# Row softmax on one core: the first two loads as one DMA each on SyncE's queue, instead of one on SyncE's and a 128/126/2-partition split on ScalarE's

## The chip, the cores and the metric

One core of a Trainium2 chip. The metric is the device time of one execution in microseconds (us), the median over the runs. Faster or slower asks for 2%. A profile is a trace of one execution; its span (first to last instruction) is about 1.4 us shorter than the device time (158.6 of 160.00 us for the kernel before).

## The reference

```
x: 16 x 1024 x 512, float32
x_scaled = x / 2.0
e = exp(x_scaled - max(x_scaled, last axis))
return e / sum(e, last axis)
```

16,384 rows of 512 values. 33.55 MB are read and 33.55 MB written, and each value gets a maximum, an exponential with its sum, and a multiplication.

## The kernel before

One tile is `r` rows for each of the 128 partitions; consecutive rows of a partition lie together in memory, so a load or store of a tile moves one piece of r x 2,048 bytes for each partition (the trace has 128 packets of 6,144 B for tile 0's load, 128 of 30,720 B for one of 15 rows). The ten tiles have 3, 7, 13 and then seven times 15 rows. They live in one arena of 98 rows, so tiles 8 and 9 take the place of tiles 0 to 3 and are loaded only after those are stored.

```
PLAN = [
    ([3], 0), ([4, 3], 3), ([5, 4, 4], 10), ([5] * 3, 23), ([5] * 3, 38), ([5] * 3, 53),
    ([5] * 3, 68), ([5] * 3, 83), ([5] * 3, 0), ([5] * 3, 15),
]
ARENA = 98
LAG = 2
SPREAD = 1
# ... cut ...
            if t == 0:
                nc.sync.dma_start(out=sb(t), in_=dram(xf, t)).then_inc(ld[t], 16)
            elif t == SPREAD:
                r = tiles[t][1] - 1
                for p, q, lo, hi in ((0, P, 0, r), (0, 126, r, r + 1), (126, P, r, r + 1)):
                    nc.scalar.dma_start(
                        out=sb(t)[p:q, lo:hi], in_=dram(xf, t)[p:q, lo:hi]
                    ).then_inc(ld[t], 16)
            else:
                nc.scalar.dma_start(out=sb(t), in_=dram(xf, t)).then_inc(ld[t], 16)
```

VectorE works in chunks (the inner lists of PLAN): the maximum of chunk k, then the multiplication of chunk k - LAG. SyncE stores a tile when its last chunk is multiplied. The loads of tiles 0 and 1 are issued ahead of the barrier that opens the program.

```
        for k in range(len(chunks) + LAG):
            if k < len(chunks):
                do_max(k)
            if k >= LAG:
                do_mul(k - LAG)
        for t in range(len(tiles)):
            nc.sync.wait_ge(s_mul, last_chunk[t] + 1)
            nc.sync.dma_start(out=dram(of, t), in_=sb(t)).then_inc(
                st[t] if t in awaited else s_end, 16
            )
```

Of the kernel before, what the change touches and what calls it, by code (L numbers as in the profile page):

```python
# [14 lines left out]
ARENA = 98  # L15
LAG = 2

SPREAD = 1

AFTER = {8: 4, 9: 5}  # L20

# [7 lines left out]
def kernel(  # L29
# [5 lines left out]
    nc = tc.nc  # L35
# [4 lines left out]
    xf = x.flatten_outer_dims()  # L40
    of = out.flatten_outer_dims()
    N, D = xf.shape
    P = nc.NUM_PARTITIONS
# [10 lines left out]
    tiles, chunks, base = [], [], 0  # L54
    for t, (cs, at) in enumerate(PLAN):
        r = sum(cs)
# [8 lines left out]
    def dram(ap, t):  # L65
        b, r, _ = tiles[t]
        return ap[b * P : (b + r) * P].rearrange("(p r) d -> p r d", r=r)

    def sb(t):
        _, r, at = tiles[t]  # L70
        return arena[:, at : at + r, :]
# [9 lines left out]
    ld = [nc.alloc_semaphore(f"ld{t}") for t in range(len(tiles))]  # L81
# [10 lines left out]
    s_max = nc.alloc_semaphore("s_max")  # L92
# [5 lines left out]
    def issue_loads(begin, end):  # L98


        for t in range(begin, end):
            if t in behind:
                continue
            if t == 0:
                nc.sync.dma_start(out=sb(t), in_=dram(xf, t)).then_inc(ld[t], 16)
            elif t == SPREAD:

                r = tiles[t][1] - 1
                for p, q, lo, hi in ((0, P, 0, r), (0, 126, r, r + 1), (126, P, r, r + 1)):
                    nc.scalar.dma_start(  # L110
                        out=sb(t)[p:q, lo:hi], in_=dram(xf, t)[p:q, lo:hi]
                    ).then_inc(ld[t], 16)
            else:
                nc.scalar.dma_start(out=sb(t), in_=dram(xf, t)).then_inc(ld[t], 16)

    def do_max(k):
        t, b, c, a = chunks[k]
        nc.vector.reduce_max(  # L118
            out=stats[:, b : b + c],
            in_=arena[:, a : a + c],  # L120
            axis=mybir.AxisListType.X,
            negate=True,
        )._wait_ge(ld[t], 48 if t == SPREAD else 16).then_inc(s_max, 1)

    def do_mul(k):
        t, b, c, a = chunks[k]
# [20 lines left out]
    def compute_and_store():  # L147
# [6 lines that stand above are left out]
# [73 lines left out]
    entry.instructions = []  # L227
    nc.switch_bb("main", None)
    issue_loads(0, 2)
    first = list(entry.instructions)  # L230
    at = next(k for k, i in enumerate(head) if type(i).__name__ == "InstDrain")
    entry.instructions = head[:at] + first + head[at:]
    act = []
    entry.instructions = list(entry.instructions) + [i for i in jumps if i not in act]
    nc.switch_body(here, parent=None, valid_engines=[i.engine for i in jumps])
    issue_loads(2, len(tiles))
    compute_and_store()

# [29 lines left out]
```

## Time and profile before

| | before |
|---|---|
| time, median of the first 3 runs | 160.02 us (159.97 to 160.12) |
| span of the profiled run | 158.6 us |
| VectorE / ScalarE busy | 131.4 / 94.4 us |
| moved by DMA | 67.13 MB, 423 GB/s over the span |

Read the busy times against the span first: no compute engine fills it. Then look at the row of DMA slices, which does. The lines are in the prediction below. The trace also records every DMA packet (queue, start, duration, size), though not the engine that moved it. On one engine a packet starts a few ns before the end of the one ahead (30,720 B packets take 1,138 ns and follow each other every 1,134), so the 16 engines can often be told apart as 16 chains; where two chains meet, they can't.

### The profile page before, as it was taken

The numbers are of one execution on the slowest core, as the hardware profiler recorded it, in microseconds if no ns is written. First come the engines' busy times: TensorE is split into PE (matmuls) and PEld (weight loads), VectorE is DVE, ScalarE is ACT, GpSimd is POOL, SyncE is SP. The second block draws the span as 40 slices with busy tenths as digits, with TensorE's granted clock in tenths as the row PEclk, the third lists the DMA queues.
The fourth block names the chain that finished last, engine by engine and source line by source line (L and its number), as shares of the span: only waits on it lengthen the run. The fifth ranks groups of instructions, "written<-read, shape, count | busy, mean of one in ns | idle before, by whom it ended". The sixth has DMA issues, their size and how long they took to land.

```text
span 158.6 us, 621 instructions
## 1 busy us (share of the span) xinstructions
DVE 131.4 (83%) x155; ACT 94.4 (60%) x257; POOL 0.2 (0%) x4
## 2 busy tenths in 40 slices
DVE  0466799999999999999999999996999389999000
ACT  0369197736874594669738797666566809763000
POOL 0000000000000000000000000000000000000000
DMA  7999999999999999999999999999999999999996
GB/s 268 449 373 430 414 431 466 435 407 399 466 443 389 434 463 448 418 444 426 442 426 434 426 426 442 426 441 411 457 395 472 395 473 395 472 395 465 395 472 263
DMA packets 3026, 67.13 MB, mean 423 GB/s; under 512 B 336, under 2 KB 336, under 8 KB 720
## 3 DMA queue, kind: packets, MB, share of 16 engines
q1 hardware_dynamic: 1584, 34.34, 50.6%
q10 hardware_dynamic: 1440, 32.77, 48.5%
q14 instruction: 2, 0.02, 0.0%
HBM read 33.55 MB, written 33.55 MB: 423 GB/s over the span
## 4 chain that ended last, share of the span: by engine, by line
DMA 52%; DVE 38%; issue 0%
DMA arena<-in_x_dram 38%; DVE stats L118 18%; DMA out_dram<-arena 14%; DVE arena L131 13%; DVE arena L138 7%; DVE recip L127 1%
## 5 line engine op out<-in xcount | busy, mean ns | idle before, releaser
L118 DVE TENSOR_REDUCE stats<-arena 128x5 f32<-128x2560 f32 (+2 forms) x27 | 72.2, 2676 | 14.6 <-DMA arena<-in_x_dram 14.6
L176 ACT ACTIVATE arena<-arena,stats 128x512 f32<-128x512 f32 x68 | 48.2, 710 | 23.4 <-DVE stats L118 23.4
L211 ACT ACTIVATE arena<-arena,stats x60 | 42.5, 710 | 20.7 <-ACTq L203 20.7
L138 DVE TENSOR_SCALAR arena<-arena,recip 128x512 f32<-128x512 f32 x93 | 38.6, 482 | 0.7
L131 DVE TENSOR_TENSOR arena<-arena,recip 128x2560 f32<-128x2560 f32 (+2 forms) x8 | 19.9, 2491 | 0.3
L176 ACT ACTIVATION_READ_ACCUMULATOR arena<-arena,stats 128x1 f32 x68 | 12.7, 187 | 0.0
L211 ACT ACTIVATION_READ_ACCUMULATOR arena<-arena,stats x60 | 11.2, 187 | 0.0
L127 DVE RECIPROCAL recip<-stats 128x5 f32<-128x5 f32 (+2 forms) x27 | 4.8, 177 | 0.0
L171 ACT ACT_TABLE_LOAD x1 | 1.3, 1283 | 5.7 <-issue 5.7
L252 POOL MEMSET const-bfloat16-1.0<- 128x1 bf16 x1 | 0.1, 101 | 0.0
L252 POOL MEMSET const-uint8-127<- 128x1 uint8 x1 | 0.1, 101 | 0.0
L252 POOL MEMSET const-float32-0.0<- 128x1 f32 x1 | 0.1, 98 | 0.2 <-issue 0.2
L252 POOL MEMSET const-float32-1.0<- 128x1 f32 x1 | 0.1, 98 | 0.0
## 6 DMA issues: line engine op xcount, KB each, us to landing
arena<-in_x_dram ACTq DMA_DIRECT2D x7, 3840.0 KB, 46.6
out_dram<-arena SPq DMA_DIRECT2D x7, 3840.0 KB, 22.7
arena<-in_x_dram ACTq DMA_DIRECT2D x1, 3328.0 KB, 14.3
out_dram<-arena SPq DMA_DIRECT2D x1, 3328.0 KB, 21.1
out_dram<-arena SPq DMA_DIRECT2D x1, 1792.0 KB, 18.2
arena<-in_x_dram ACTq DMA_DIRECT2D x1, 1536.0 KB
arena<-in_x_dram SPq DMA_DIRECT2D x1, 768.0 KB, 6.2
out_dram<-arena SPq DMA_DIRECT2D x1, 768.0 KB, 15.8
```

The source lines that it names most:

```text
L118: nc.vector.reduce_max(out=stats[:, b : b + c], in_=arena[:, a : a + c], axis=mybir.AxisListType.X, negate=True,)._wait_ge(ld[t], 48 if t ...
L127: nc.vector.reciprocal(out=recip[:, b : b + c], in_=stats[:, b : b + c])._wait_ge(s_exp, k + 1).then_inc(s_rec, 1)
L131: nc.vector.tensor_mul(out=arena[:, a : a + c], in0=arena[:, a : a + c], in1=recip[:, b : b + c].unsqueeze(2).to_broadcast([P, c, D]),)._w ...
L138: ins = nc.vector.tensor_scalar_mul(out=arena[:, a + r], in0=arena[:, a + r], scalar1=recip[:, b + r : b + r + 1],)
L171: nc.scalar.preload_act_table(mybir.ActivationFunctionType.Exp)
L176: ins = nc.scalar.activation(out=arena[:, a + r], in_=arena[:, a + r], func=mybir.ActivationFunctionType.Exp, bias=stats[:, b + r : b + r ...
L211: ins = nc.scalar.activation(out=data, in_=data, func=mybir.ActivationFunctionType.Exp, bias=stat, scale=0.5, accum_out=stat,)
L252: nc = _bacc.Bacc("TRN2", target_bir_lowering=False, num_devices=1)
```

## The change

The intent: tile 0 first and undisturbed, tile 1 behind it on the same queue, and whole rows, with one DMA for each load in place of three for tile 1.

The constant SPREAD goes, and HALVES = 1 comes in its place:

```diff
             if t == 0:
+                for p in range(HALVES):          # HALVES = 1
+                    nc.sync.dma_start(
+                        out=sb(t)[p:P:HALVES], in_=dram(xf, t)[p:P:HALVES]
+                    ).then_inc(ld[t], 16)
+            elif t == 1:
                 nc.sync.dma_start(out=sb(t), in_=dram(xf, t)).then_inc(ld[t], 16)
-            elif t == SPREAD:
-                r = tiles[t][1] - 1
-                for p, q, lo, hi in ((0, P, 0, r), (0, 126, r, r + 1), (126, P, r, r + 1)):
-                    nc.scalar.dma_start(
-                        out=sb(t)[p:q, lo:hi], in_=dram(xf, t)[p:q, lo:hi]
-                    ).then_inc(ld[t], 16)
             else:
                 nc.scalar.dma_start(out=sb(t), in_=dram(xf, t)).then_inc(ld[t], 16)
@@ the wait of the maximum
-        )._wait_ge(ld[t], 48 if t == SPREAD else 16).then_inc(s_max, 1)
+        )._wait_ge(ld[t], 16 * HALVES if t == 0 else 16).then_inc(s_max, 1)
```

More of the change, by code (lines that the diff above doesn't have):

```diff
@@ L16 @@
 LAG = 2
-SPREAD = 1
+HALVES = 1
 AFTER = {8: 4, 9: 5}
```

## The prediction

> **What bounds the kernel now.** I read the page from the top: the busy shares, then the slices, then the DMA queues.
>
> ```profile
> span 158.6 us, 621 instructions
> DVE 131.4 (83%) x155; ACT 94.4 (60%) x257; POOL 0.2 (0%) x4
> ...
> DVE  0466799999999999999999999996999389999000
> ...
> DMA  7999999999999999999999999999999999999996
> ...
> DMA packets 3026, 67.13 MB, mean 423 GB/s; under 512 B 336, under 2 KB 336, under 8 KB 720
> ...
> q1 hardware_dynamic: 1584, 34.34, 50.6%
> q10 hardware_dynamic: 1440, 32.77, 48.5%
> ```
>
> No compute engine is full; VectorE has holes at the start, at slices 27 and 31 and after the last multiply. The 16 DMA engines have none between first and last slice. q1 is SyncE's queue (33.55 MB of stores and the 0.79 MB of tile 0), q10 ScalarE's (the other loads). Second view: the stretches.
>
> ```profile
> core 0: us, DVE busy (x) ACT busy (x) POOL busy (x), PEclk, DMA share, GB/s
> 0.00:1.00 1.00, 0.00 (x0) 0.00 (x0) 0.20 (x4) 1.00 0.04 6
> 1.00:3.00 2.00, 0.00 (x0) 0.00 (x0) 0.00 (x0) 1.00 0.98 338
> 3.00:20.00 17.00, 10.04 (x10) 8.71 (x22) 0.00 (x0) 1.00 1.02 422
> 20.00:60.00 40.00, 39.76 (x23) 27.53 (x76) 0.00 (x0) 1.00 1.01 431
> 60.00:126.00 66.00, 62.49 (x91) 47.11 (x130) 0.00 (x0) 1.00 1.01 433
> 126.00:157.00 31.00, 19.11 (x33) 11.07 (x32) 0.00 (x0) 1.00 1.00 431
> ```
>
> The last two columns carry it: share 1.00 or more and 431 to 433 GB/s, whether loads and stores mix (20 to 126) or stores run alone (126 to 157). So the kernel is 1.0 us to the first packet, then 67.1 MB through full DMA engines, then a landing. Only bytes, the start, the balance among the 16 engines, or a hole in the DMA can move the end. Third view: the timeline of the part that the change touches, and of the end.
>
> ```profile
> 0.00 0.38 SPq L105 DMA_DIRECT2D arena<-in_x_dram  x1
> 0.12 1.36 ACTq L110 DMA_DIRECT2D arena<-in_x_dram  x3
> ...
> 2.65 3.07 ACTq L114 DMA_DIRECT2D arena<-in_x_dram  x6
> ...
> 6.22 1.75 DVE L118 TENSOR_REDUCE stats<-arena 128x3 f32<-128x1536 f32 x1 [6.22 <-DMA arena<-in_x_dram]
> ...
> 9.27 3.94 DVE L118 TENSOR_REDUCE stats<-arena 128x4 f32<-128x2048 f32 x2 [1.30 <-DMA arena<-in_x_dram]
> ...
> 14.65 0.34 SPq L158 DMA_DIRECT2D out_dram<-arena  x1
> ...
> 16.99 2.82 DVE L118 TENSOR_REDUCE stats<-arena 128x5 f32<-128x2560 f32 x1 [2.37 <-DMA arena<-in_x_dram]
> ```
> ```profile
> 127.66 2.82 DVE L118 TENSOR_REDUCE stats<-arena 128x5 f32<-128x2560 f32 x1 [3.29 <-DMA arena<-in_x_dram]
> ```
> ```profile
> 137.64 9.67 SPq L158 DMA_DIRECT2D out_dram<-arena  x2
> ```
>
> Tile 0 can be used at 6.22, tile 1 at 9.27, tile 2 at 16.99; the first store is issued at 14.65. At the end VectorE waits 3.29 us for the last load, works 19.3 us without a pause, and the last store is issued at 146.98 (137.64 + 9.67 - 0.33). In the trace's packet records that store's first packet starts at 148.41, on the heels of the store before it. From issue to first packet on an empty queue took 1.0 us (first load: 0.00 to 1.00), so the last store could be about 0.4 us later before a hole opens: the slack at the end is small. The chain of waits passes through VectorE and two long DMAs (store of tile 3, load of tile 9); I don't take it for the bound, because those DMAs mostly stand in queues behind others: the load of tile 9 is issued at 81.5, and its first packet is at 108.8.
>
> [...] ScalarE's queue has 160 four-byte completion packets, which is 9 DMAs x 16 + 14 + 2. The odd split is thus no accident: two engines carry none of the 128 last rows of tile 1. [...] while tile 0 is stored beside a load, one engine's store packets (6,144 B) follow each other every 1.365 us, which is one of 230 ns plus one 30,720 B packet of 1,135 ns. [...]
>
> **The change part by part.**
>
> Rows. A 2,048 B packet goes out every 80 ns on its engine, a 12,288 B one every 457, a 14,336 B one (tile 1's store has them) every 531. Tile 1's load costs most engines 8 x 457 + 9 x 80 = 4.38 us before (two of them 10 rows, 4.46), and the two spared ones 8 x 457 = 3.66. After, all have 8 x 531 = 4.25. So 14 engines gain 0.13 to 0.21 and two lose 0.59; the mean gains (12 x 0.13 + 2 x 0.21 - 2 x 0.59)/16 = 0.05 us, nothing.
>
> Why it was split: in tile 0's load 14 engines start between 1.00 and 1.25 us, the other two only at 1.73 and 1.75. Behind the split the two without rows begin tile 2 at 7.69 and 7.79, the others at 7.70 to 8.27: over-compensated. After, I move these: the late two to about 8.29 and 8.40, the others to 7.57 to 8.14. The latest engine of the start goes from 8.27 to 8.40.
>
> What that does at the end: the engines' last packets end at 157.48 to 157.95, and two at 158.14 and 158.19. These two had a detour of 309 ns each (8,192 B fetches of instructions, at 28.08 and 71.28). Followed back packet by packet, with some ambiguity, they are not the spared two, which end near 157.5 to 157.6. After: fetching engines 158.19 - 0.13 = 158.06; spared ones 157.5 to 157.6 + 0.59 = 158.1 to 158.2. The latest is again about 158.15 (before 158.19). Sum: 0.0 us, at most a few tenths.
>
> Order. Tile 0 no longer shares the engines with tile 1: 8 packets of 230 ns after a slow first one end at about 3.1 (3.6 on the late two); with the 0.36 us that the last landing took before, its reduce starts near 4.0 instead of 6.22. Tile 1 follows on the same queue. ScalarE no longer issues three loads ahead of the opening barrier, where its arrival was the last (1.76 us); the six loads should be issued near 1.9 instead of 2.65, and tile 2's packets come in turn with tile 1's from about 4.5. Tile 1 then has about 5 packets left at 531 + 988 ns a turn: 7.6 us, so it lands near 13 (12.3 to 14), where it was 9.27. The reduces of tile 1 (3.94 us) and the multiply of tile 0 (1.45 us) stand before everything else on VectorE: the first store goes out near 18.6 instead of 14.65, and VectorE begins tile 2 near 18.6 instead of 16.99.
>
> Off the path: meanwhile the loads keep all engines full, so the bytes not stored from 18 to 22 us are loaded instead. VectorE's 1.6 us are absorbed by its two waits for loads (1.42 at 108 us, 3.29 at 124). The store queue starts about 4 us later, but before it had two small gaps between the first three stores (28.8 to 30.4 and 43.1 to 45.2) which more backlog closes, giving back about 2.7. Net, loads lead by a little: the last one lands about 126 instead of 127.6, and the last store is issued at 145.5 to 147. The slack at the end grows or stays; the end does not move.
>
> **The rivals.** (1) The spared engines were in fact the ones that set the end, or a fetch falls on one of them: the end is then 158.15 + 0.6, that is +0.5 us, 160.5. For it: the author went to the trouble of such a split. Against: my tracing. (2) A new wait: tile 1's delay of 4 us shifts VectorE, the last load or the last store by more than the 0.4 us of slack; each us beyond costs a us, so 161. Against: two waits of VectorE and a leading load queue lie between. (3) A hole in the DMA after tile 0, if SyncE's second DMA came too late: its issue at about 0.45 us plus 1.0 to 1.7 is before 3.1, so no. (4) A gain: the start loses 0.9 to 1.4 us on each engine against its packets' plain sum (15.1 us from the first packet to the end of tile 2, where 14.1 are accounted for), some of it while two queues mix small packets (460 to 650 ns for packets that otherwise take 460). In-order loads may save 0.2 to 0.3: 159.7.
>
> **Range and chances.** No part reaches 1 us on the path: sum 0.0, rival 1 up by 0.5, rival 4 down by 0.3; two per cent would be 3.2 us. Predicted 160.0 us, range 159.5 to 160.6; faster 0.01, within 2% 0.97, slower 0.02.
>
> **What would show it.** First reduce near 4.0, second near 13, first store near 18.6, barrier and ScalarE's loads near 1.9; DMA slices full throughout; 320 completion packets instead of 336, none of 2,048 B; last store issued no later than 147.4, its first packet directly behind the store before it; the last packets of the 16 engines ending between 157.4 and 158.3. Wrong would be: a DMA slice under 9 in the middle, a last store with a pause ahead of its packets, or one or two engines that end 0.5 us after all others.

The sum came to 0.0 us. One step rested on a rule alone: that no rate above the 433 GB/s of the middle stretch was to be had, which no run here shows. The row counts stand on the trace of before: beside nine DMAs with 16 completion packets each, ScalarE's queue has 16 more for the 126 + 2 rows, and two engines carry none of these rows (their last 12,288 B packets end at 7.684 and 7.790 us, tile 2's first ones start at 7.686 and 7.792). The ten rows on two engines are an estimate: 128 rows shared evenly by the other 14 are nine each and two over.

## The result, and the profile after

160.34 us (160.26 to 160.46, 4 runs) against 160.05 us (159.97 to 160.12, 4 runs): ratio 1.0019, 95% interval 1.0002 to 1.0037. The ratio is the mean time of one kernel's runs over that of the other's in the same rounds, so not quite the ratio of the medians. By the 2% measure it is the same time; the 0.3 us are small, but the interval leaves out 1.

The page of the changed kernel, the lines that answer to those in the prediction:

```profile
span 159.0 us, 619 instructions
DVE 131.2 (83%) x155; ACT 94.4 (59%) x257; POOL 0.2 (0%) x4
...
DVE  0405999999999999999999999999999699995000
...
DMA  7999999998999999999999999999999999999996
...
DMA packets 2882, 67.13 MB, mean 422 GB/s; under 512 B 320, under 2 KB 320, under 8 KB 576
```

The DMA row is still full, with one 8 near 38 us. VectorE now has a hole at slices 2 and 3 and fewer later. The 16 missing completion packets (320, not 336) are those of the split. The timeline of the changed kernel, its beginning and its end (start and duration in us, then what ran):

```profile
0.00 0.38 SPq L106 DMA_DIRECT2D arena<-in_x_dram  x1
...
0.43 0.42 SPq L110 DMA_DIRECT2D arena<-in_x_dram  x1
1.92 2.94 ACTq L112 DMA_DIRECT2D arena<-in_x_dram  x6
4.49 1.75 DVE L116 TENSOR_REDUCE stats<-arena 128x3 f32<-128x1536 f32 x1 [4.49 <-DMA arena<-in_x_dram]
...
13.69 3.95 DVE L116 TENSOR_REDUCE stats<-arena 128x4 f32<-128x2048 f32 x2 [7.45 <-DMA arena<-in_x_dram]
...
18.95 2.82 DVE L116 TENSOR_REDUCE stats<-arena 128x5 f32<-128x2560 f32 x1
19.06 0.35 SPq L156 DMA_DIRECT2D out_dram<-arena  x1
```
```profile
126.03 2.82 DVE L116 TENSOR_REDUCE stats<-arena 128x5 f32<-128x2560 f32 x1 [1.22 <-DMA arena<-in_x_dram]
```
```profile
136.01 9.67 SPq L156 DMA_DIRECT2D out_dram<-arena  x2
```

Tile 0 comes 1.7 us sooner (4.49, before 6.22), tile 1 comes 4.4 us later (13.69, before 9.27), and the first store goes out 4.4 us later (19.06, before 14.65). At the end it has all been made up: the last load is there at 126.03 instead of 127.66, and the last store is issued at 145.35 (136.01 + 9.67 - 0.33) instead of 146.98. Its first packet is at 148.48, 3.1 us after the issue, and the store ahead starts its last packet at 148.35, so it waited in a queue that never ran empty. Nothing on VectorE decides the end in either kernel; the DMA engines do.

So the 0.3 us must be in how the DMA engines work. The stretches of before, then of the changed kernel (stretch, length, busy times, clock; the last two columns are DMA share and GB/s):

```profile
1.00:16.00 15.00, 7.06 (x7) 7.91 (x20) 0.00 (x0) 1.00 1.01 402
16.00:46.00 30.00, 28.81 (x18) 18.92 (x53) 0.00 (x0) 1.00 1.01 430
```
```profile
1.00:16.00 15.00, 4.06 (x3) 3.51 (x7) 0.00 (x0) 1.00 1.04 431
16.00:46.00 30.00, 29.79 (x21) 21.81 (x60) 0.00 (x0) 1.00 0.99 413
46.00:157.00 111.00, 97.36 (x133) 69.09 (x190) 0.00 (x0) 1.00 1.01 434
```

The changed kernel starts better, 431 instead of 402 GB/s, and gives it back from 16 to 46 us, 413 instead of 430. The share of busy time doesn't tell it (0.99 at 413 GB/s, 1.01 at 430): a packet that takes longer counts as busy all the while. From the packet records I worked out a time lost per engine: a packet's undisturbed spacing (230 ns for 6,144 B, 531 for 14,336, 987 for 26,624, 1,134 for 30,720, 80 for 2,048) is what it should use, and what a stretch holds beyond the sum of these, over 16 engines, is lost. I also took the end of each engine's last packet.

| trace | lost 1 to 16 us | lost 16 to 46 | lost 46 to 157 | mean end | latest end |
|---|---|---|---|---|---|
| before | 1.21 | 0.29 | 0.07 | 157.74 | 158.19 |
| changed | 0.76 | 1.00 | 0.04 | 157.93 | 158.56 |

Start -0.45, middle +0.71, sum with the rest +0.23; whole rows need a little less time (0.05 us on the mean, by the same spacings), so the mean end moved by +0.19. The latest engine was 0.45 us behind the mean and is now 0.63 behind: another 0.18. Together they are the +0.37 between these two executions. (Two copies of one kernel differ too; see the repeats.)

### The profile page after: what moved, and what is told of

It is laid out like the page before. It is cut to its first block, busy times and chain, and to the rows that moved or that the text cites. A ratio compares the mean times of both kernels' runs of the same rounds, so it can differ in the third digit from the quotient of the medians.

```text
span 159.0 us, 619 instructions
## 1 busy us (share of the span) xinstructions
DVE 131.2 (83%) x155; ACT 94.4 (59%) x257; POOL 0.2 (0%) x4
## 4 chain that ended last, share of the span: by engine, by line
DMA 49%; DVE 42%; issue 0%; SPq 0%
DMA arena<-in_x_dram 35%; DVE stats L116 21%; DMA out_dram<-arena 15%; DVE arena L129 13%; DVE arena L136 7%; DVE recip L125 1%; SPq L106 0%
```

## The experiments

Theory A: only the balance counts; two engines are late by themselves, the split relieved them, and now they set the end. Theory B: the later first stores meet the loads at a worse time, and the loss in the middle is what was added. Ten kernels ran, each with 5 rounds.

**The changed kernel once more.** No edit.

> The changed kernel once more, for its interval and a second trace. In the first trace the engines' last packets end at 157.93 us on the mean (before 157.75) and the latest two at +0.63 (before +0.44). Theory A (balance: the two engines without rows in the split are late by themselves and now set the end) and theory B (the later stores make load packets run longer at 22 to 26 and 34 to 38 us: 0.3 and 0.5 us lost per engine there, where before lost 0.0 and 0.2) both expect 160.3 us. B expects the stretched packets at the same places again; if they are elsewhere or gone, B's loss is chance of one execution.

Measured 160.49 us (160.35 to 160.65) against 160.06, ratio 1.0027 (1.0014 to 1.0040). Lost 0.78, 0.95 and 0.05 in the three stretches; mean end 157.91, latest 158.62. The stretched packets are at the same places: 0.27 lost at 22 to 24 us, 0.14 and 0.38 at 34 to 38. So the loss belongs to the schedule, and the kernel is slower by 0.2 to 0.3%.

**The kernel before once more.** No edit.

> The kernel before once more, for a second trace and for how far two copies of one kernel differ in this measure. 160.05 us, ratio within 0.1%. If the time lost per engine on longer packets falls where it fell before (0.5 us between 6 and 12 us, 0.05 at 30 to 32, 0.15 at 36 to 40), it belongs to the schedule and not to one execution; the mean end of the engines is then again near 157.75 and the latest at +0.44.

Measured 160.14 us, ratio 0.9998 (0.9984 to 1.0011). Lost 1.18, 0.40 and 0.09: again at the start (0.41 between 6 and 12 us) and little in the middle. But the mean end is 157.84 and the latest 158.49, where I expected 157.75 and 158.19. Loss and its places repeat; the end of the latest engine differs by 0.3 us between two executions of one kernel. The two pairs of traces put the middle at +0.55 to +0.71 and the mean end at +0.07 to +0.19; of the latest engine's part a single trace can't be trusted to more than a sign.

**Tile 1 whole, left on ScalarE's queue** (the kernel before with one part of the change; the wait for tile 1 goes from 48 to 16 with it):

```diff
-            elif t == SPREAD:
-                ...three DMAs of 128, 126 and 2 partitions...
             else:
                 nc.scalar.dma_start(out=sb(t), in_=dram(xf, t)).then_inc(ld[t], 16)
```

> The kernel before, but tile 1 whole in one DMA, still on ScalarE's queue beside tile 0. A (balance alone): as the changed kernel, 160.3 us, the two late engines 0.6 us behind the mean. B: stores start as early as before, so no loss in the middle; mean end at 157.7, and the late pair at most at 158.2 to 158.4: 160.0 to 160.2 us.

Measured 160.13 us (160.09 to 160.53) against 160.06, ratio 1.0013 (1.0000 to 1.0026). Its stretches:

```profile
1.00:16.00 15.00, 7.06 (x7) 8.54 (x21) 0.00 (x0) 1.00 1.04 431
16.00:46.00 30.00, 29.24 (x18) 18.73 (x52) 0.00 (x0) 1.00 1.00 415
```

The time is where B put it, but not for B's reason. The start is as good as the changed kernel's: the whole tile alone brings the 431 GB/s, and the queue does nothing for it. Tile 1 can be used at 8.65 us here, at 13.69 from SyncE's queue in the changed kernel. The packets show where it was lost. With the split, the first 26,624 B packet of tile 2 took 1,341 to 1,485 ns on every engine (1,281 to 1,446 in the second trace), and 987 ns on every engine here. It is not simply the packet behind a small row that gets slow: the two engines that carry no 2,048 B row went from a 12,288 B packet straight to tile 2, and theirs took 1,485 and 1,445 ns, the longest of all. What in the split does it, the rows on the other engines or three DMAs in place of one, no run here separates. And 0.93 us are lost in the middle although the first store is issued at 14.02, as early as before. So "later stores lose more" is too simple. A doesn't hold as stated either: the latest engine was 0.41 us behind the mean (158.27 against 157.86), not 0.6. In time, this kernel and the changed one can't be told apart (1.0013 against 1.0019 and 1.0027, with intervals that overlap), so no cost of the new order alone is shown.

**The split kept, but on SyncE's queue in order** (the changed kernel with the other part undone):

```diff
             elif t == 1:
-                nc.sync.dma_start(out=sb(t), in_=dram(xf, t)).then_inc(ld[t], 16)
+                r = tiles[t][1] - 1
+                for p, q, lo, hi in ((0, P, 0, r), (0, 126, r, r + 1), (126, P, r, r + 1)):
+                    nc.sync.dma_start(
+                        out=sb(t)[p:q, lo:hi], in_=dram(xf, t)[p:q, lo:hi]
+                    ).then_inc(ld[t], 16)
```

> The changed kernel, but tile 1 is split again into 128x6 rows and 126 + 2 rows, now on SyncE's queue in order. A (balance alone): the late pair is relieved of 0.6 us, the time goes back to that of before, 160.05 us. B (later stores): the mean loss of the middle stays, and only the 0.2 us of the late pair come back: 160.15 to 160.25, mean end of the engines still near 157.9, largest deviation 0.4 or less.

Measured 164.38 us (163.68 to 165.05) against 160.06, ratio 1.0262 (1.0237 to 1.0287). Both theories missed it by 4 us, and it can't tell them apart. The page's slices of VectorE and DMA, and VectorE's timeline at tile 1:

```profile
DVE  0400049999999999999999999999999999999400
...
DMA  7999998999999999999999999999999999088988
```
```profile
22.76 3.95 DVE L120 TENSOR_REDUCE stats<-arena 128x4 f32<-128x2048 f32 x2 [16.51 <-DMA arena<-in_x_dram]
```

The small rows now stand in a queue that takes turns with the loads of tiles 2 and 3: each 2,048 B row, nine or ten on each of 14 engines, waits for a 26,624 B or 30,720 B packet (in the kernel before, too, one store packet and one load packet alternate on an engine, every 1.365 us), and the last of them ends at 21.12 us. Tile 1 can be used at 22.76 instead of 13.69. From there VectorE never rests and yet comes too late: the DMA engines stand still at 139 to 144 us (the 0 in slice 34) until the next store is issued at 143.77. This is the prediction's second rival, made large. The delay of 4.4 us in the changed kernel was absorbed; one of 13.5 us (22.76 against 9.27) was not.

**The split in the last store instead:**

(the last wait counts two more DMAs)

```diff
+            if t == len(tiles) - 1:
+                ...the same 128, 126 and 2 partitions, as three stores...
+                continue
             nc.sync.dma_start(out=dram(of, t), in_=sb(t)).then_inc(
```

> The changed kernel with the same 128 + 126 + 2 split put into the last row of the last store instead. The two engines that carry none of its 2,048 B packets are seen in the trace at the end itself. A and B: they are the pair that ended last (158.56), now at about 157.9, the others at +0.08: the end is set by the next ones, 158.3 to 158.4, and the time is 160.15 us. If the latest pair is another one (fetches of instructions), the end stays or grows by 0.1: 160.35 to 160.45.

Measured 160.17 us (160.08 to 160.40), ratio 1.0004 (0.9991 to 1.0017), in the same rounds in which the changed kernel had 160.49. The packets tell the pair: 14 engines' last large packet is followed by 2,048 B rows, two engines' is not, and these two finish their large packets last of all 16 (157.98 us; the next 157.90, the mean 157.37). So the pair without rows in such a split is the pair that is last in this kernel, and with the split it is not. The gain itself stands on the times alone: the traced execution, the slowest of its five (160.40 us), ends at 158.62 like the changed kernel's second trace, and not at the 158.3 to 158.4 expected.

**Tile 0 multiplied and stored before tile 1 is awaited:**

```diff
             if k < len(chunks):
                 do_max(k)
-            if k >= LAG:
+            if k == 0:
+                do_mul(0)
+            if k > LAG:
                 do_mul(k - LAG)
```

> The changed kernel, but VectorE multiplies tile 0 before it waits for tile 1, so tile 0's store is issued near 10 us instead of 19.06 and its packets follow the load of tile 1 directly, from about 12.4 us. Theory B (load packets are stretched where the first stores meet the loads, so it depends on their time): the loss at 22 to 26 us moves to 12 to 16 or vanishes, and so may that at 34 to 38; mean end between 157.4 and 157.9 against 157.93, time 159.9 to 160.3. Rival B2 (the loss belongs to a place in the stream of loads, or to a moment): losses stay at 22 to 26 and 34 to 38, mean end and time as the changed kernel, 160.35.

**Tile 0 stored later:**

```diff
-            nc.sync.wait_ge(s_mul, last_chunk[t] + 1)
+            nc.sync.wait_ge(s_mul, max(last_chunk[t] + 1, 2))
```

> The changed kernel, but tile 0's store waits for the multiply of the next chunk too, so it is issued near 24.3 us instead of 19.06. B: the loss at 22 to 26 moves to about 27 to 31 us or changes its size, and the second one moves with it; time 160.1 to 160.7. B2: losses stay at 22 to 26 and 34 to 38, 160.35 us. A hole at the end is not expected: the changed kernel's last store had some 3 us in hand (issued at 145.35, first packet at 148.48).

The early one measured 160.16 us (160.07 to 160.46), ratio 1.0001 (0.9987 to 1.0015); the late one 160.25 us (160.14 to 160.33), ratio 1.0008 (0.9994 to 1.0022). First store issued at 10.00 and at 24.22. First the early one's stretches, then the late one's:

```profile
1.00:16.00 15.00, 5.42 (x7) 3.51 (x7) 0.00 (x0) 1.00 1.02 407
16.00:46.00 30.00, 29.70 (x20) 22.39 (x62) 0.00 (x0) 1.00 1.00 427
```
```profile
1.00:16.00 15.00, 4.04 (x3) 3.50 (x7) 0.00 (x0) 1.00 1.04 431
16.00:46.00 30.00, 29.80 (x21) 21.82 (x60) 0.00 (x0) 1.00 0.99 420
```

| trace | first store issued | lost 1 to 16 us | lost 16 to 46 | lost 46 to 157 | mean end |
|---|---|---|---|---|---|
| stored early | 10.00 | 1.23 | 0.33 | 0.24 | 157.94 |
| changed | 19.06 | 0.76 | 1.00 | 0.04 | 157.93 |
| stored later | 24.22 | 0.75 | 0.53 | 0.33 | 157.74 |

The loss moves with the stores: 0.44 us at 12 to 16 us in the early one and none at 22 to 26; from 26 to 34 and 46 to 60 us in the late one. The rival, that it belongs to a place in the stream of loads, falls, since nothing is lost at 22 to 26 in either. But a good part of it only moves. The early one's profiled execution was its slowest (160.46 us), so its mean end reads high.

**Tile 0 in two DMAs of 64 rows:** `HALVES = 2`.

> The changed kernel with tile 0 in two DMAs of 64 rows each (every second row). The late pair started tile 0 at 1.81 and 1.88 us where the others started at 1.05 to 1.24. If that lag comes from the number of rows of the first DMA (the pair is served last), it halves: the pair starts near 1.4 to 1.5 us, is 0.3 us behind the mean at the end instead of 0.63, and the time is 160.1 to 160.2. If the lag is the same for a DMA of any size, 160.35 us or, with the second issue's 0.4 us in front of tile 1, up to 160.5.

Measured 161.16 us (161.00 to 161.43), ratio 1.0068 (1.0054 to 1.0082). Two stretches of its start, then the same two of the changed kernel:

```profile
1.00:3.00 2.00, 0.00 (x0) 0.00 (x0) 0.00 (x0) 1.00 0.83 261
3.00:6.00 3.00, 1.37 (x1) 0.00 (x0) 0.00 (x0) 1.00 0.81 265
```
```profile
1.00:3.00 2.00, 0.00 (x0) 0.00 (x0) 0.00 (x0) 1.00 0.93 329
3.00:6.00 3.00, 1.51 (x1) 1.11 (x1) 0.00 (x0) 1.00 1.09 444
```

A pair starts late here too, at 1.98 and 1.99 us, where the others start at 1.32 to 1.64 (in the changed kernel the others started at 1.05 to 1.44, not 1.24 as the expectation has it). But its first packets are short (234 and 258 ns, the others' 534 to 834), and the lag is soon gone: the engines end the first half within 0.27 us of each other, where the changed kernel's pair ended tile 0 0.64 and 0.70 behind the mean. At the end the latest engine is 0.66 us behind the mean all the same (159.25 against 158.59); it may be the one that ended tile 0 only at 4.31, where the others were done by 3.87. And three issues of 545 to 585 ns each put tile 1's first packet at 3.61 instead of 3.13, the DMA engines have a real hole at 3 to 6 us (265 GB/s), and 2.24 us are lost in the start instead of 0.76. A hole at the start is on the path; my expectation allowed 0.15 us for it. The time grew by 0.7 to 0.8 us and not by 1.5, because the middle lost far less than the changed kernel's (413 GB/s there):

```profile
16.00:46.00 30.00, 29.79 (x22) 21.81 (x60) 0.00 (x0) 1.00 1.00 430
```

Its first store was issued at 19.44, only 0.38 us later than the changed kernel's 19.06. So the loss in the middle hangs on small shifts, not on early or late as such.

**Two combinations**, in search of a better version: the early multiplication with the split in the last store, and tile 1 whole on ScalarE's queue with the split in the last store. Their edits are those shown above.

> Both helps together on the changed kernel: tile 0 multiplied and stored early (alone 160.16 us) and the last row of the last store split over 126 and 2 partitions (alone 160.17). If the two act on different terms (loss where stores meet loads; the late pair at the end), they add up: 0.2 us + 0.2 us off 160.4, that is 159.95 to 160.05 us. If each only shifts the same few tenths, 160.15.

> Tile 1 whole on ScalarE's queue beside tile 0 (alone 160.13 us) with the split in the last row of the last store. Its late pair ended at +0.40, close to the next ones (+0.32, +0.22), and the split costs the other 14 engines 0.1 us: 160.05 to 160.2 us, no clear gain. If the relief is worth as much as on the changed kernel (0.2 us), 159.95.

Measured 160.32 us (160.06 to 160.68), ratio 1.0016 (1.0004 to 1.0028), and 160.43 us (160.24 to 161.05), ratio 1.0023 (1.0009 to 1.0038). Nothing adds up; both are a little slower than before, and their medians are above those of their parts, though the intervals overlap. So what the split in the last store is worth, 0.3 us in one comparison, is not shown to be a gain that lasts. None of the ten kernels beats the one before.

## Why the prediction was right or wrong

The main step held: the DMA engines bound both kernels (busy share 0.99 to 1.04 in the stretches 1 to 16, 16 to 46 and 46 to 157 us), and neither tile 1's delay nor VectorE's moves the end. The predicted 160.0 us was 0.34 off, inside the range of 159.5 to 160.6. That it came so near is in part luck: two terms of about half a us, one at the start and one in the middle, were not in the sum, and they nearly cancel. Of the prediction's own signs of being wrong one came true, a DMA slice of 8 near 38 us, and the last packets ended at 157.56 to 158.56, not by 158.3.

The order part held nearly line by line. ScalarE's loads were issued at 1.92 (about 1.9 predicted), the second reduce was at 13.69 (near 13), the first store at 19.06 (near 18.6), the last load there at 126.03 (about 126), the last store issued at 145.35 (145.5 at the earliest), with its packets directly behind those ahead. The first reduce was at 4.49 and not near 4.0: I let the late pair end tile 0 at 3.6 us, and it ended at 4.05 and 4.12.

The sum "0.0" was wrong by 0.3 us, in these terms:

- "The mean gains ... 0.05 us, nothing". I priced the split by its rows' own 80 ns. With it, tile 2's first packet took 1,341 to 1,485 ns instead of 987 on all engines, also on the two without such rows. Taking the split away gained 0.45 us at the start, shown by the whole tile on ScalarE's queue. The fourth rival had the sign and half the size, but not the reason: the gain came without the loads in order.
- No step allowed for a loss in the middle. I took "431 to 433 GB/s" there for a constant, which was an estimate; with other times of the first stores it was 413. This cost 0.55 to 0.71 us, more than the start gained. That it moves with the stores is shown; that tile 1 whole on ScalarE's queue loses as much with an early store shows that it isn't lateness as such.
- "The latest is again about 158.15". It was 158.56 and, in the second trace, 158.62. The step that failed is the lag of 0.5 us that I gave the pair (it was 0.6 to 0.7) and, as far as the changed kernel shows, "Followed back ... the spared two, which end near 157.5 to 157.6". The first rival, that the spared pair sets the end, had the right pair for the changed kernel; which pair is last in the kernel before, no run marked. Its +0.5 was too much, because before too the latest engine was 0.45 to 0.65 us behind the mean.

What stays open: why load packets get longer, by some 0.2 to 0.35 us each on the mean of such a moment, when the first stores take turns with them (in the changed kernel 1,426 ns on the mean at 22 to 24 us, 1,342 and 1,470 at 34 to 38, where 30,720 B otherwise take 1,138). It is not seen from 60 us on, where both queues carry 30,720 B packets (the loads' mean is 1,138 ns there, 1,139 in the kernel before); no run here separates the sizes of the packets from the places they read and write.

## What to carry to other kernels

While the DMA engines are full from the first packet to the last, ask of a later load only whether the delay eats up the slack of the engine behind it: here a delay of 4.4 us cost 0.4 us at most, and one of 13.5 us cost 4.3. A hole at the start is on the path: 1.5 us more were lost there, and the time grew by 0.7 to 0.8. A split into small rows is to be priced by a run and not by its bytes, and by what it takes turns with: the same 126 + 2 rows went with 0.45 us lost at the start of the kernel before, and with 4.3 us where each had to wait for a large packet.
